# Taking the wide elementwise work off GpSimd in a two-block chain: splits and convolution on VectorE, stick-breaking masks by matmul, the gated branch first

## The chip, the cores and the metric

The kernel runs on one core of a Trainium2 chip. The metric is device time in microseconds (us). Before the change the median of three runs is 1020.0 us (1019.26 to 1021.23). A profile records one execution on the chip, instruction by instruction, for the engines PE (TensorE; PEld is its weight load), DVE (VectorE), ACT (ScalarE), POOL (GpSimd) and SP (SyncE, which issues the DMAs).

## The reference, cut to what matters

Two blocks over 256 tokens of width 1024, in fp32. The first is a mixing layer with a feed-forward layer; the second has a retention layer and a differential attention layer, each with a convolutional feed-forward layer. The change touches the mixing layer, and the way in which all weights are prepared.

```python
h = _rmsnorm(x, g_attn)
p = h @ w_in            # columns: a_b, a_c, a_h (256 each), b_glu (512), q, k, v (512 each)
y_a = a_b * _causal_dwconv(a_c * a_h, w_conv_a)                       # 3 taps
g = b_glu[..., :256] * jax.nn.sigmoid(b_glu[..., 256:])
g = _causal_dwconv(g, w_conv_b) + b_conv_b                            # 31 taps
y_b = jax.nn.silu(_layernorm(g, ln_b_g, ln_b_b))
# stick-breaking attention, 8 heads of 64, for each block of 128 queries:
z = einsum(q, k) * scale
mask = s_idx < t_idx
log_beta = log_sigmoid(z)
log_1m = where(mask, log_beta - z, 0.0)
suffix = cumsum(log_1m, reverse) - log_1m
a = where(mask, exp(log_beta + suffix), 0.0)
y_c = a @ v
x = x + concatenate([y_a, y_b, y_c]) @ w_out
```

## The kernel before

**Weights and matmuls.** All weights are packed into 322 units of 128 x 1024 numbers, loaded in pairs by SP into `raw`. Each unit is split into two fp32r parts: ACT copies it to `hi`, and `raw - hi` becomes `lo` (`split_one`, lines 374 to 397). The products are formed as hi·hi + hi·lo + lo·hi, three matmuls for each. A ring of 8 unit pairs (`RING`) holds split units; a unit's slot is free again when its last matmul has been issued. A unit comes in one of three forms: `ws` (the weights are stationary, 256 tokens move: 24 matmuls of 256 columns, result as [channel, token]; `wstat`, line 520), `xs` (activations stationary, 512 weight columns move, result as [token, channel]; four units make 512 columns, 48 matmuls of 512 columns; `xstat_tokens` and `xstat`, lines 550 to 572) and `kt` (the down projections, also 512 columns; `Down`, line 588).

**The order of instructions.** `Flow` (lines 147 to 213) is a planner that runs when the kernel is built. Each operation has a priority (CHAIN, ATT, EVAC, SPLIT, IDLE, MAIN, in this order) and an estimated cost in ns; whenever an engine is free by these estimates it takes the most urgent operation whose inputs are there. The instructions are then fixed in that order: on the chip each engine runs its list strictly in order. All vector, scalar and matmul instructions are recorded through line 200 (`kick` calls them at line 200), so the views have to be read by tile names.

**Who makes `lo`.** By `split_one`, DVE makes it with one subtraction of 1024 columns (two of 512 while a phase border is being crossed or in the fine part of the attention), unless DVE's backlog by the plan is larger than POOL's by a margin (`SPILL` 1200 ns, `HELD_SPILL` -1500 ns, `FINE_SPILL` 0); then POOL makes it in four pieces of 256 columns. 28 of the units go to POOL.

**The mix phase** (`mix_phase`, line 645) takes 22 units of `w_in` in this order: V (four `xs` units), GLU (four `ws` units, two channel blocks), four head pairs (`q` and `k`, one `ws` unit each), y_a (six `ws` units); then 8 `kt` units of `w_out` in the order of `MIX_KT`: the four head pairs' channels, y_a's first, y_b's two, y_a's second. `Down` computes token block 0 for all eight, and token block 1 for seven of them afterwards (`TAIL`), while the residual and the norm of token block 0 (`chain`) are already on their way.

- *Convolution of 31 taps* (`conv_b`, `conv_pool`, lines 734 to 767): the first channel block's 31 taps and 8 of the second's are on DVE, one instruction each, with priority IDLE; 23 taps of the second block are on POOL, two instructions each (a scaled copy into `tap`, an addition into `part`). Norm (`norm`) and swish (`swish`) follow; they end with `y_ready[2]` and `y_ready[3]`.
- *Stick-breaking* (`stick`, line 821), for one pair of heads: scores into two PSUM banks (fp32 matmuls), two sigmoids on ACT to `gam` (1 - beta) and two to `beta`, in strips of 388 columns with spare columns between the blocks; POOL masks both with `affine_select` (two each) and clears one column; DVE forms the running product from the right by `tensor_tensor_scan` over `gam` and `one`, then `beta * run`; PE transposes (`at0`, `at1`), and `sb_av` multiplies with V into `yp`. `gam` and `run` exist once, `beta` twice.
- PSUM has 8 banks, handed out first come first served (`Slots`).

Each phase border has a chain of its own: residual, sum of squares (ACT), the reciprocal root by a power of -0.5 on one column (POOL, `rstd_of`, line 440), scaling (DVE, `big`), transposes, and the split of the activations.

Of the kernel before, what the change touches and what calls it, by code (L numbers as in the profile page):

```python
# [11 lines left out]
F32R = mybir.dt.float32r  # L12
AF = mybir.ActivationFunctionType
# [4 lines left out]
P = 128  # L18
# [16 lines left out]
SPILL = 1200.0  # L35
WARM = 20
HALVED = 6
POOL_TAPS = 23
HELD_CHUNKS = 2
FINE_SPILL = 0.0  # L40
URGENT = 8
HELD_SPILL = -1500.0
# [13 lines left out]
SBW = 388  # L56
COS0, SIN0, DEC0, ONE0, TRI0 = 0, 256, 512, 2048, 2048 + 2 * SBW
NCONST = TRI0 + P

MIX_KT = [4, 5, 6, 7, 0, 2, 3, 1]  # L60
# [12 lines left out]
def plan():  # L73
# [73 lines left out]
class Flow:  # L147
    """Orders the instructions: each engine takes the most urgent operation whose inputs are there,
    by estimated costs, and the instructions are traced in that order."""
# [57 lines left out]
    def backlog(self, engine):  # L207
        return max(0.0, self.free.get(engine, 0.0) - self.now) + sum(o.cost for _, _, o in self.queue.get(engine, []))

# [6 lines left out]
class Slots:  # L216
    """Counts the buffers of one tag."""
# [26 lines left out]
class Acts:  # L244
    """Activations as [channel, token], split into two parts, and when they are there."""
# [17 lines left out]
def chain_kernel(ctx: ExitStack, tc: tile.TileContext, x_in, wpack, gains, chan, small_rows, consts, out):  # L263
# [66 lines left out]
    def tp(p, pairs):  # L330
        return pe(p, 107 * len(pairs), [(nc.tensor.transpose, (dst, src, ident), {}) for dst, src in pairs])
# [42 lines left out]
    def split_one(i, src, left):  # L374
        hi, lo = unit_at[i]
        while state["hold"] is not None and i >= state["pos"] + KEEP:
            yield state["hold"]
        held = state["hold"] is not None
        n = HELD_CHUNKS if held or state["fine"] else 1
        w = D // n  # L380
        for c in range(n):
            o = act(SPLIT, hi[:, c * w:c * w + w], src[:, c * w:c * w + w], AF.Copy)
        yield o
        if flow.backlog("dve") > flow.backlog("pool") + (HELD_SPILL if held else FINE_SPILL if state["fine"] else SPILL):
            for c in range(4):
                cs = slice(c * 256, c * 256 + 256)
                o = pool(SPLIT, 690, nc.gpsimd.tensor_tensor, lo[:, cs], src[:, cs], hi[:, cs].bitcast(F32), op=ALU.subtract)
            yield o
        else:
            for c in range(n):  # L390
                cs = slice(c * w, c * w + w)
                o = tt(SPLIT, lo[:, cs], src[:, cs], hi[:, cs].bitcast(F32), ALU.subtract)
            yield o
        left[0] -= 1
        if not left[0]:
            raw.put()
        flow.fire(unit_done[i])
# [29 lines left out]
    junk = cpool.tile([P, 512], mybir.dt.bfloat16, tag="junk", name="junk")  # L427
# [92 lines left out]
    def wstat(dst, w, sx):  # L520
# [3 lines left out]
        for k in range(KD):  # L524
            if k % 4 == 0:
                yield sx.ready[0][k // 4]
                yield sx.ready[1][k // 4]
            o = pe(MAIN, 325, [
                mm(dst, h3[:, k, :], sx.hi[:, k, :], k == 0, False),
                mm(dst, h3[:, k, :], sx.lo[:, k, :], False, False),  # L530
                mm(dst, l3[:, k, :], sx.hi[:, k, :], False, k == KD - 1)])
            yield o.end
# [3 lines left out]
    def xstat_mm(dst, u, j, t, sx):  # L536
        hi, lo = u
        tsl = slice(t * P, (t + 1) * P)
        for kk in range(2):
# [3 lines left out]
            o = pe(MAIN, 645, [  # L543
# [30 lines left out]
    def down_mm(acc, n, i, t, u, y):  # L574
# [6 lines left out]
        for d, cs in ((a, c0), (b, c1)):  # L581
            o = pe(MAIN, 645, [mm(d, yh[:, tsl], hi[:, cs], first, False), mm(d, yh[:, tsl], lo[:, cs], False, False),
                               mm(d, yl[:, tsl], hi[:, cs], False, last)])
            yield o.end
            both.append(o)
# [59 lines left out]
    def mix_phase(mp):  # L645
# [25 lines left out]

        def late_loads():
            yield raw_seen2
            cop = load(ch, chan, P * NCH * 4)
            oop = load(one, consts[:, ONE0:ONE0 + 2 * SBW], P * 2 * SBW * 4)
            yield cop
            yield oop
        raw_seen2 = pair_seen[3]
# [8 lines left out]
        for beta in betas:  # L687
            nc.gpsimd.memset(beta[:, :, 386:388], 0.0)
        nc.gpsimd.memset(gam[:, :, 386:388], 0.0)
# [11 lines left out]
        yield from xstat_tokens("w_in", sx, [v_evac])  # L701

# [5 lines left out]
        sgs = slots(mp, 1, [P, S], F32, "sg")  # L708
# [9 lines left out]
        glus = []  # L718
        for c in range(2):
            p0, p1 = yield from banks.get(2)  # L720
            yield from wstat(p0[:, :S], "w_in", sx)
            o = yield from wstat(p1[:, :S], "w_in", sx)
            glus.append(flow.spawn(glu(c, p0, p1, o)))
# [3 lines left out]
        part = mp.tile([P, S], F32, tag="part", name="part")  # L727
        taps = [mp.tile([P, S], F32, tag=f"tap{n}", name=f"tap{n}") for n in range(2)]

        def pool_tap(j, out, s2):  # L730
            w = ch[:, CB0 + 31 + j:CB0 + 32 + j]
            return pool(IDLE, 460, nc.gpsimd.tensor_scalar, out, gpad[:, 1, j:j + S], w, s2, op0=ALU.mult, op1=ALU.add)

        def conv_pool():
            o = pool_tap(0, part, 0.0)
            prev = None
            for j in range(1, POOL_TAPS + 1):
                if j < POOL_TAPS:
                    o = pool_tap(j, taps[j % 2], 0.0)
                if prev is not None:  # L740
                    o = pool(IDLE, 690, nc.gpsimd.tensor_tensor, part, part, prev, op=ALU.add)
                prev = taps[j % 2]
                yield o.end
            yield o

        def conv_b():
# [7 lines left out]
            started = set()  # L754
            o = None
            for c, j in todo:
                if o is not None:
                    yield o.end
                w = ch[:, CB0 + 31 * c + j:CB0 + 31 * c + j + 1]
                if c not in started:  # L760
                    started.add(c)
                    o = ts(IDLE, cb[:, c, :], gpad[:, c, j:j + S], w, ch[:, BB0 + c:BB0 + c + 1], ALU.mult, ALU.add)
                else:
                    o = stt(IDLE, cb[:, c, :], gpad[:, c, j:j + S], w, cb[:, c, :], ALU.mult, ALU.add)
            yield o
            yield other
            yield tt(EVAC, cb[:, 1, :], cb[:, 1, :], part, ALU.add)
# [40 lines left out]
        def sb_av(i, j, at, yp, beta, v_ok):  # L808
            cs = slice(j * 64, j * 64 + P)
            yield tp(ATT, [(at[:, b * P:(b + 1) * P], beta[:, j, c0:c0 + P]) for b, c0 in enumerate((0, 130, 258))])  # L810
# [10 lines left out]
        def stick(i, pr):  # L821
# [3 lines left out]
            scs = yield from banks.get(2)  # L825
            sops = []
            for j in range(2):
                rows = slice(j * 64, j * 64 + 64)
                sops.append(pe(ATT, 650, [mm(scs[j][:, 0:130], q[rows, 0:P], k[rows, 0:130], True, True),
                                          mm(scs[j][:, 130:386], q[rows, P:S], k[rows, :], True, True)]))  # L830
            yield from bgr.get()
            beta = yield from bbeta.get()
            for j in range(2):
# [3 lines left out]
                a = act(ATT, gam[:, j, 0:386], scs[j][:, 0:386], AF.Sigmoid, scale=-0.125)  # L837
                b = act(ATT, beta[:, j, 0:386], scs[j][:, 0:386], AF.Sigmoid, scale=0.125)
            yield a

            def mask(tile_, b0, fill):
                return pool(ATT, 362, nc.gpsimd.affine_select, out=tile_[:, :, b0:b0 + P], in_=tile_[:, :, b0:b0 + P],
                            pattern=[[0, 2], [-1, P]], compare_op=ALU.is_gt, fill=fill, base=0, channel_multiplier=1)

            g_ops = [mask(gam, 0, 1.0), mask(gam, 258, 1.0), pool(ATT, 100, nc.gpsimd.memset, gam[:, :, 128:129], 0.0)]
            yield b
            banks.put(2)
            b_ops = [mask(beta, 0, 0.0), mask(beta, 258, 0.0)]
# [3 lines left out]
            for o in g_ops:  # L852
                yield o
            yield consts_in
# [4 lines left out]
            for o in b_ops:  # L859
                yield o  # L860
# [18 lines left out]
        for i in range(4):  # L879
# [6 lines left out]
            flow.spawn(stick(i, pr))  # L886

# [561 lines left out]
def _constants():  # L1449
# [14 lines left out]
    for h in range(2):  # L1464
        c[:, ONE0 + h * SBW + 128] = 1.0
        c[:, ONE0 + h * SBW + 386] = 1.0
    q = np.arange(P)
    c[:, TRI0:TRI0 + P] = np.where(q[None, :] <= q[:, None], 0.0, -1e30)
    return c
# [26 lines left out]
```

## Time and profile before

| | |
|---|---|
| median of three runs | 1020.0 us |
| span of the profiled execution, first to last instruction | 1016.7 us |
| mean granted TensorE clock | 0.990 |
| DVE `lo<-raw,hi` 128x1024 | 288 x 1245 ns |
| POOL `lo<-raw,hi` 128x256 | 112 x 1021 ns |
| POOL `tap<-gpad,ch` and `part<-part,tap` | 22 x 1063 ns and 22 x 873 ns |
| POOL masks of `gam` and of `beta` | 8 x 424 ns and 8 x 1136 ns |
| DVE scan `run<-gam,one` | 4 x 1945 ns |

The profiled execution has no time of its own beside its span; the span lies 3.3 us under the median of the runs. In the page, the busy share of an engine is an average over the whole span. A line of the timeline has the start, the duration, the engine, the line, the operation, output<-inputs and, in brackets, the idle time of the engine before it and what ended that. A matmul's duration is longer than the step to the next one, since matmuls are pipelined: PE's pace is read from starts.

### The profile page before, as it was taken

To read this page: it belongs to the slowest core of one execution; us is meant where nothing else is said; L and a number is where in the kernel's file an instruction comes from. 1 tells how busy PE (TensorE), PEld (TensorE's weight loads), DVE (VectorE), ACT (ScalarE), POOL (GpSimd) and SP (SyncE) were. 2 spreads that over 40 slices of the span, in tenths; PEclk is the share of its full clock that TensorE was granted. 3 is DMA by queue.
4 is the path that set the end of the run, shared out by engine and by line. 5 is a ranking of instruction groups with operands and counts; after the bars stand their busy time and mean duration, and the time that the engine had idled before them with its cause. 6 is when DMAs were issued, how large, how long until landed. Compare 5 with 4: busy or idle time off the path is not lost.

```text
span 1016.7 us, 15598 instructions
## 1 busy us (share of the span) xinstructions
PE 986.9 (97%) x6144; PEld 880.4 (87%) x6144; DVE 688.9 (68%) x1010; ACT 561.3 (55%) x948; POOL 191.4 (19%) x232
## 2 busy tenths in 40 slices
PE   8977999999999999999999999999999999999997
PEld 6966878999997989898879999998899779999996
DVE  5798666555557676565379866666777579766663
ACT  5633456444435545445368555556767768555551
POOL 1497060000007010000062100005200262100000
PEclk9978999999999999999999999999999999999999
DMA  8712347455544744545347555553653246555531
GB/s 299 284 43 90 139 166 289 169 205 171 201 167 162 273 134 174 199 154 178 135 166 269 208 171 203 172 202 129 206 212 125 83 166 228 208 174 199 172 119 42
DMA packets 28441, 180.07 MB, mean 177 GB/s; under 512 B 3152, under 2 KB 4304, under 8 KB 8528
## 3 DMA queue, kind: packets, MB, share of 16 engines
q1 hardware_dynamic: 28368, 179.08, 49.8%
q8 instruction: 48, 0.79, 0.3%
q14 instruction: 25, 0.20, 0.1%
HBM read 178.02 MB, written 1.05 MB: 176 GB/s over the span
## 4 chain that ended last, share of the span: by engine, by line
PE 67%; issue 18%; POOL 9%; DVE 2%; ACT 1%; DMA 1%; SPq 0%; POOLq 0%; DVEq 0%; ACTq 0%
PE bank L200 67%; POOL lo L200 5%; POOL tap L200 2%; POOL part L200 1%; POOL tiny L200 1%; DMA raw<-wpack 1%; ACT hi L200 1%; DVE lo L200 1%; POOL beta L200 0%; DVE big L200 0%; DVE run L200 0%; POOL gam L200 0%; ACT junk L200 0%; DVE x L200 0%; DVE beta L200 0%
## 5 line engine op out<-in xcount | busy, mean ns | idle before, releaser
L200 DVE TENSOR_TENSOR lo<-raw,hi 128x1024 fp32r<-128x1024 f32 (+1 forms) x300 | 369.8, 1238 | 129.7 <-ACT hi L200 129.0
L200 ACT ACTIVATE hi<-raw 128x1024 fp32r<-128x1024 f32 (+1 forms) x344 | 340.5, 1002 | 144.6 <-PE bank L200 125.7
L200 PE MATMUL bank<-xh,hi 128*128 128x256 f32 x1104 | 316.2, 286 | 0.0
L200 PE MATMUL bank<-xh,lo 128*128 128x256 f32 x1104 | 313.3, 284 | 0.0
L200 PE MATMUL bank<-xl,hi 128*128 128x256 f32 x1104 | 313.2, 284 | 0.0
L200 PEld LDWEIGHTS bank<-xh,hi 128*128 128x128 f32 x1104 | 212.6, 193 | 3.9 <-issue 1.3
L200 PEld LDWEIGHTS bank<-xl,hi 128*128 128x128 f32 x1104 | 212.5, 192 | 2.5
L200 PEld LDWEIGHTS bank<-xh,lo 128*128 128x128 f32 x1104 | 212.3, 192 | 0.0
L200 POOL TENSOR_TENSOR tiny<-tiny,mhalf 128x1 f32<-128x1 f32 (+1 forms) x40 | 25.1, 629 | 708.7 <-DVE tiny L200 708.7
L200 POOL TENSOR_TENSOR lo<-raw,hi 128x256 fp32r<-128x256 f32 x112 | 110.7, 1021 | 86.4 <-ACT hi L200 85.0
L200 PE MATMUL bank<-hi,xh 128*128 128x512 f32 x272 | 108.2, 398 | 0.0
L200 DVE SCALAR_TENSOR_TENSOR cv<-bank,ch,cv 128x254 f32<-128x254 f32 (+1 forms) x176 | 72.5, 474 | 51.8 <-ACT cv L200 51.6
L200 PE MATMUL bank<-lo,xh 128*128 128x512 f32 x272 | 106.5, 391 | 0.8 <-DVE lo L200 0.8
L200 PE MATMUL bank<-hi,fh 128*128 128x512 f32 x272 | 106.9, 393 | 0.0
L200 PE MATMUL bank<-hi,xl 128*128 128x512 f32 x272 | 106.7, 392 | 0.1
L200 PE MATMUL bank<-lo,fh 128*128 128x512 f32 x272 | 106.5, 392 | 0.0
L200 PE MATMUL bank<-hi,fl 128*128 128x512 f32 x272 | 105.9, 389 | 0.0
L200 ACT ACTIVATE cv<-bank,ch 128x256 f32<-128x256 f32 x88 | 44.2, 561 | 61.7 <-PE bank L200 61.7
L200 PEld LDWEIGHTS bank<-lo,xh 128*128 128x128 f32 x272 | 51.2, 188 | 12.0 <-DVE lo L200 1.9
L200 PEld LDWEIGHTS bank<-hi,xl 128*128 128x128 f32 x272 | 51.1, 188 | 12.0 <-DVE xl L200 1.4
L200 PEld LDWEIGHTS bank<-hi,fl 128*128 128x128 f32 x272 | 51.1, 188 | 11.0
L200 PEld LDWEIGHTS bank<-hi,xh 128*128 128x128 f32 x272 | 51.2, 188 | 9.7 <-ACT xh L200 0.2
(170 smaller groups left out, 1188.9 us busy)
## 6 DMA issues: line engine op xcount, KB each, us to landing
raw<-wpack SPq DMA_DIRECT2D x155, 1024.0 KB, 4.9
big<-gains SPq DMA_DIRECT2D x12, 512.0 KB, 6.7
raw<-wpack SPq DMA_DIRECT2D x12, 512.0 KB, 7.5
x<-x SPq DMA_DIRECT2D x4, 256.0 KB, 5.8
out_dram<-x SPq DMA_DIRECT2D x4, 256.0 KB, 2.1
dec<-consts SPq DMA_DIRECT2D x4, 192.0 KB, 5.2
one<-consts SPq DMA_DIRECT2D x1, 388.0 KB, 6.0
ch<-chan SPq DMA_DIRECT2D x1, 213.5 KB, 5.5
```

The lines of the kernel that those rows point to most:

```text
L200: fn(*a, **k)
```

## The change

- *Splits*: every `lo` is made on DVE; the choice between DVE and POOL, with its margins and `backlog`, is gone.
- *Order of `w_in`*: GLU is first and now has the form `xs` (512 columns, result as [token, channel]); V comes after the second head pair (`V_AFTER = 1`) and uses `xstat`, which holds two banks.
- *GLU*: sigmoid and product for each token block, then two PE transposes and an ACT copy into `gpad`; two buffers `sg` instead of one.
- *Convolution*: all 62 taps on DVE, channel blocks in turn.
- *Masks*: after each pair's scores, a bf16 matmul of an identity with a tile that has 0 below the diagonal and -1e30 on and above it adds the mask to the scores' two diagonal blocks in PSUM. The sigmoids then give 1 for `gam` and 0 for `beta` there. Strips are 384 columns wide; the scan's second operation is `max`, with ones at the blocks' ends. POOL's masks and clears are gone.
- *Costs in the plan*: a group of three 256-column matmuls 358 ns instead of 325, of three 512-column matmuls 681 instead of 645, the scan 1860 instead of 880, transposes 96 each and 90 more instead of 107 each.

POOL keeps the powers of one or two columns and the clears at the start.

```diff
 def plan():
-    xs("w_in", 2304)
-    for c in (768, 1024, 896, 1152):
-        ws("w_in", c)
+    xs("w_in", 768)
     for i in range(4):
         ws("w_in", 1280 + i * P)
         ws("w_in", 1792 + i * P)
+        if i == V_AFTER:
+            xs("w_in", 2304)
...
 def split_one(i, src, left):
-        if flow.backlog("dve") > flow.backlog("pool") + (HELD_SPILL if held else FINE_SPILL if state["fine"] else SPILL):
-            for c in range(4):
-                cs = slice(c * 256, c * 256 + 256)
-                o = pool(SPLIT, 690, nc.gpsimd.tensor_tensor, lo[:, cs], src[:, cs], hi[:, cs].bitcast(F32), op=ALU.subtract)
-            yield o
-        else:
-            for c in range(n):
+        for c in range(n):
+            cs = slice(c * w, c * w + w)
+            o = tt(SPLIT, lo[:, cs], src[:, cs], hi[:, cs].bitcast(F32), ALU.subtract)
+        yield o
...
-        def glu(c, p0, p1, o):
+        def glu(t, d, o):
             yield o
             sg = yield from sgs.get()
-            yield act(EVAC, sg, p1[:, :S], AF.Sigmoid)
-            yield tt(EVAC, gpad[:, c, 30:], p0[:, :S], sg, ALU.mult)
-            banks.put(2)
+            yield act(EVAC, sg, d[:, S:], AF.Sigmoid)
+            yield tt(EVAC, sg, d[:, :S], sg, ALU.mult)
+            banks.put()
+            pt = yield from banks.get()
+            yield tp(EVAC, [(pt[:, c * P:(c + 1) * P], sg[:, c * P:(c + 1) * P]) for c in range(2)])
             sgs.put()
+            yield act(EVAC, gpad[:, :, 30 + t * P:30 + (t + 1) * P], pt[:, :S].rearrange("p (c s) -> p c s", c=2), AF.Copy)
...
         def conv_b():
-            other = flow.spawn(conv_pool())
-            todo = [(0, j) for j in range(31)]
-            for n, j in enumerate(range(POOL_TAPS, 31)):
-                todo.insert(3 * n + 1, (1, j))
+            for j in range(31):
+                for c in range(2):
...
         def stick(i, pr):
+            yield consts_in
             for j in range(2):
-                sops.append(pe(ATT, 650, [mm(scs[j][:, 0:130], q[rows, 0:P], k[rows, 0:130], True, True),
-                                          mm(scs[j][:, 130:386], q[rows, P:S], k[rows, :], True, True)]))
+                pe(ATT, 435, [mm(scs[j][:, 0:P], q[rows, 0:P], k[rows, 0:P], True, False),
+                              mm(scs[j][:, P:SBW], q[rows, P:S], k[rows, :], False, False)])
+            for j in range(2):
+                diag = scs[j].rearrange("p (b c) -> p b c", b=2)[:, :, 0:P]
+                sops.append(pe(ATT, 130, [mm(diag, identb, trib.rearrange("p (a c) -> p a c", a=1).broadcast_to([P, 2, P]), False, True)]))
...
-            g_ops = [mask(gam, 0, 1.0), mask(gam, 258, 1.0), pool(ATT, 100, nc.gpsimd.memset, gam[:, :, 128:129], 0.0)]
-            b_ops = [mask(beta, 0, 0.0), mask(beta, 258, 0.0)]
-            yield flow.op("dve", ATT, 880, [(nc.vector.tensor_tensor_scan, (rf[:, ::-1], gf[:, ::-1], one[:, ::-1], 0.0),
-                                             {"op0": ALU.mult, "op1": ALU.add})])
+            s_op = flow.op("dve", ATT, 1860, [(nc.vector.tensor_tensor_scan, (rf[:, ::-1], gf[:, ::-1], one[:, ::-1], 0.0),
+                                             {"op0": ALU.mult, "op1": ALU.max})])
```

More of the change, by code (lines that the diff above doesn't have):

```diff
@@ L330, in tp @@
     def tp(p, pairs):
-        return pe(p, 107 * len(pairs), [(nc.tensor.transpose, (dst, src, ident), {}) for dst, src in pairs])
+        return pe(p, 96 * len(pairs) + 90, [(nc.tensor.transpose, (dst, src, ident), {}) for dst, src in pairs])
     def split_to(p, hi, lo, src):
@@ L377, in split_one @@
             yield state["hold"]
[L378 to L379 removed]
+        n = HELD_CHUNKS if state["hold"] is not None or state["fine"] else 1
         w = D // n
@@ L670, in mix_phase @@
         one = mp.tile([P, 2 * SBW], F32, tag="one", name="one")
+        tri = mp.tile([P, P], F32, tag="tri", name="stri")
         def late_loads():
@@ L675, in late_loads @@
             oop = load(one, consts[:, ONE0:ONE0 + 2 * SBW], P * 2 * SBW * 4)
+            top = load(tri, consts[:, TRI0 + P:TRI0 + 2 * P], P * P * 4)
             yield cop
             yield oop
+            yield top
+            act(EVAC, identb, ident, AF.Copy)
+            yield act(EVAC, trib, tri, AF.Copy)
         raw_seen2 = pair_seen[3]
@@ L686, in mix_phase @@
         bbeta = Slots(flow, 2, lambda: free_betas.pop(0))
-        for beta in betas:
-            nc.gpsimd.memset(beta[:, :, 386:388], 0.0)
-        nc.gpsimd.memset(gam[:, :, 386:388], 0.0)
+        trib = mp.tile([P, P], BF16, tag="trib", name="trib")
+        identb = mp.tile([P, P], BF16, tag="identb", name="identb")
         vp = mp.tile([P, 2, 4, 192], F32, tag="vp", name="vp")
@@ L707, in mix_phase @@
         nc.gpsimd.memset(gpad[:, :, 0:30], 0.0)
-        sgs = slots(mp, 1, [P, S], F32, "sg")
-        def glu(c, p0, p1, o):
+        sgs = slots(mp, 2, [P, S], F32, "sg")
+        glus = [Ev(), Ev()]
+        def glu(t, d, o):
             yield o
             sg = yield from sgs.get()
-            yield act(EVAC, sg, p1[:, :S], AF.Sigmoid)
-            yield tt(EVAC, gpad[:, c, 30:], p0[:, :S], sg, ALU.mult)
-            banks.put(2)
-            sgs.put()
[L718 to L723, printed above, removed]
+            yield act(EVAC, sg, d[:, S:], AF.Sigmoid)
[3 more added lines that the diff above has]
+            yield tp(EVAC, [(pt[:, c * P:(c + 1) * P], sg[:, c * P:(c + 1) * P]) for c in range(2)])
+            sgs.put()
+            yield act(EVAC, gpad[:, :, 30 + t * P:30 + (t + 1) * P], pt[:, :S].rearrange("p (c s) -> p c s", c=2), AF.Copy)
+            banks.put()
+            flow.fire(glus[t])
+        yield from xstat_tokens("w_in", sx, [glu])
         cb = mp.tile([P, 2, S], F32, tag="cb", name="cb")
         xn = gpad[:, :, 0:S]
[L727 to L744, printed above, removed]
         def conv_b():
@@ L836, in stick @@
                     qks.put(2)
[L837 to L843, printed above, removed]
-            g_ops = [mask(gam, 0, 1.0), mask(gam, 258, 1.0), pool(ATT, 100, nc.gpsimd.memset, gam[:, :, 128:129], 0.0)]
-            yield b
-            banks.put(2)
-            b_ops = [mask(beta, 0, 0.0), mask(beta, 258, 0.0)]
+                a = act(ATT, gam[:, j, :], scs[j][:, 0:SBW], AF.Sigmoid, scale=-0.125)
+                b = act(ATT, beta[:, j, :], scs[j][:, 0:SBW], AF.Sigmoid, scale=0.125)
             gf = gam.rearrange("p j c -> p (j c)")
```

61 lines of the change are left out of this document (25 added, 36 removed).

## The prediction

> **What bounds the kernel now.** I read the page first: the span, the busy shares, the granted clock by slices and the chain that ended last.
>
> ```profile
> span 1016.7 us, 15598 instructions
> PE 986.9 (97%) x6144; PEld 880.4 (87%) x6144; DVE 688.9 (68%) x1010; ACT 561.3 (55%) x948; POOL 191.4 (19%) x232
> ...
> PEclk9978999999999999999999999999999999999999
> ...
> PE 67%; issue 18%; POOL 9%; DVE 2%; ACT 1%; DMA 1%; SPq 0%; POOLq 0%; DVEq 0%; ACTq 0%
> ```
>
> PE carries the kernel, and its clock dips in one place, the third and fourth of 40 slices. POOL, busy for a fifth of the span, holds 9% of the chain. Next, the stages of the mix phase by busy time:
>
> ```profile
> 25.96:38.26 12.30, 12.30 (x104) 12.30 (x104) 7.85 (x8) 8.81 (x11) 0.00 (x0) 1.00 0.90 309
> 38.26:98.20 59.94, 45.98 (x321) 42.07 (x320) 52.98 (x63) 25.48 (x47) 54.30 (x65) 0.86 0.30 108
> ...
> 110.98:123.60 12.62, 12.62 (x57) 10.16 (x56) 5.83 (x11) 2.43 (x3) 0.00 (x0) 1.00 0.50 202
> 123.60:145.00 21.40, 20.85 (x101) 16.71 (x100) 15.22 (x20) 13.83 (x25) 17.47 (x18) 1.00 0.45 154
> ```
>
> The columns are PE, PEld, DVE, ACT, POOL, clock, DMA. From 38.26 (first convolution tap) to 98.20 (last) PE is idle for 14.0 of 59.94 us, while POOL (54.30) and DVE (52.98) are almost full. The waits of 40 to 100 us, and one head pair in the timelines of PE and DVE, show why:
>
> ```profile
> PE bank L200 <- DVE beta L200: 14.0, 4, 4.6
> ...
> DVE run L200 <- POOL gam L200: 6.2, 4, 2.2
> ```
>
> ```profile
> 50.68 0.93 PE L200 MATMUL bank<-qk,qk 64*128 64x130 f32 x8
> 55.44 1.54 PE L200 MATMUL bank<-ident,beta 128*128 128x128 f32 x6 [3.83 <-DVE beta L200]
> ```
>
> ```profile
> 51.29 1.94 DVE L200 TENSOR_TENSOR_SCAN run<-gam,one 128x776 f32<-128x776 f32 x1 [1.39 <-POOL gam L200]
> 53.15 1.35 DVE L200 TENSOR_TENSOR lo<-raw,hi 128x1024 fp32r<-128x1024 f32 x1
> 54.43 0.95 DVE L200 TENSOR_TENSOR beta<-beta,run 128x775 f32<-128x775 f32 x1
> ```
>
> The scan waits for the masks, which POOL makes between its taps, the product for the scan, and the transposes, put into PE's order by a planner that charges 880 ns for a scan of 1.94 us, hold up every weight matmul behind them. Four such holes are all of the 14.0 us. The clock of 0.86 means that 28% of 59.94 us, 16.8 us, went by at half speed.
>
> **PE's share of the stage.** The steps of PE at full clock, from its timeline: 29 matmuls of 512 columns (19.21 to 25.57), 153 of 256 columns (25.79 to 44.02), scores, and a stretch of six transposes, nine weight matmuls and eight value matmuls (95.87 to 98.96):
>
> ```profile
> 19.21 0.39 PE L200 MATMUL bank<-lo,xh 128*128 128x512 f32 x1
> 25.57 0.39 PE L200 MATMUL bank<-hi,xl 128*128 128x512 f32 x1
> 25.79 0.28 PE L200 MATMUL bank<-xh,hi 128*128 128x256 f32 x1
> ```
>
> ```profile
> 44.02 0.28 PE L200 MATMUL bank<-xh,lo 128*128 128x256 f32 x1
> 44.23 0.93 PE L200 MATMUL bank<-qk,qk 64*128 64x130 f32 x8
> 45.10 0.38 PE L200 MATMUL bank<-xh,hi 128*128 128x256 f32 x1
> ```
>
> ```profile
> 95.87 0.88 PE L200 MATMUL bank<-ident,beta 128*128 128x128 f32 x6 [2.80 <-DVE beta L200]
> 98.96 0.60 PE L200 MATMUL bank<-ident,cb 128*128 128x128 f32 x4
> 99.31 0.36 PE L200 MATMUL bank<-xh,hi 128*128 128x256 f32 x1
> ```
>
> A start-to-start step is 6.36/28 = 0.227 us for 512 columns and 18.23/152 = 0.120 for 256; a pair's scores cost 0.87, its transposes and values 3.09 - 9 x 0.120 = 2.0, four transposes 0.35. The stage from 25.79 to the first `w_out` matmul at 110.98 lasts 85.2 us. Its work at full speed is 18 units x 24 x 0.120 = 51.8, four pairs x 2.9 = 11.6, eight later transposes 0.7: 64.1 us. So 21 us are lost here, 14.0 in holes and about 7 to the half clock.
>
> Changed, GLU takes V's place ahead of 25.79. Behind it stand 14 units x 2.88 = 40.3, V as four 512-column units 48 x 0.227 = 10.9, pairs 11.6, eight mask matmuls of 256 columns, GLU's four transposes 0.35 and 0.7. The masks are in bf16, which the trace doesn't show: 0.120 each by the f32r row, up to 0.22 by the fp32 scores (eight matmuls of 128 and 256 columns in 0.87); I take 0.120, 1.0 in all. Sum 64.9: the floor for the start of `w_out` is 90.7, a gain of 20.3. ACT, busy for 25.48 of 59.94 us, has room for V's moved evictions and GLU's new copy. One hole I expect: V wants two banks while two pairs hold three each (`at0`, `at1`, `yp`), that is all eight, and `q` of pair 2 is queued behind V's eviction. I put 1.5 us there (0 to 3): 92.2.
>
> **DVE's share.** What it must do until the convolution is done decides the rest. Its rows between 26 and 124 us, then taps (four of the same kind, in the conv phase, POOL idle) and splits back to back without POOL beside them:
>
> ```profile
> L200 DVE TENSOR_TENSOR lo<-raw,hi 128x1024 fp32r<-128x1024 f32 x23 | 29.5, 1297 | 4.4 <-ACT hi L200 4.4
> L200 DVE SCALAR_TENSOR_TENSOR cb<-gpad,ch,cb 128x256 f32<-128x256 f32 x37 | 25.7, 715 | 0.4
> ```
>
> ```profile
> 579.93 1.65 DVE L200 SCALAR_TENSOR_TENSOR cv<-bank,ch,cv 128x255 f32<-128x255 f32 x4 [1.67 <-ACT cv L200]
> 581.50 1.21 DVE L200 TENSOR_TENSOR lo<-raw,hi 128x1024 fp32r<-128x1024 f32 x1
> ```
>
> ```profile
> 33.11 3.50 DVE L200 TENSOR_TENSOR lo<-raw,hi 128x1024 fp32r<-128x1024 f32 x3 [0.52 <-ACT hi L200]
> 37.92 0.42 DVE L200 TENSOR_TENSOR gpad<-bank,sg 128x256 f32<-128x256 f32 x1 [1.31 <-ACT sg L200]
> 38.26 0.40 DVE L200 TENSOR_SCALAR cb<-gpad,ch 128x256 f32<-128x256 f32 x1
> ```
>
> A tap costs 0.715 us beside POOL and 1.57/4 = 0.39 alone: the 62 taps on DVE alone cost 24.2 us, less than the 25.7 that 37 cost now. POOL's share of the convolution was paid by slowing DVE. Alone, a split costs (3.50 - 1.21)/2 = 1.14.
>
> The first tap now starts at 38.26. With GLU ahead its last matmul starts at 25.57; product, transposes and a copy follow, an estimate of 28.5. From there to the last tap DVE does: taps 24.2; about 21 splits (23 between 26 and 124 now, none of them POOL's) 23.9; four scans x 1.86 (51.29 to 53.15) 7.4; four products x 0.95 = 3.8; `yl` and half of conv_a, ten small steps at 0.35 (an estimate between taps and the 0.42 row), 3.5. Sum 62.8. Now DVE is busy for 52.98 of 59.94 and waits 6.2 for POOL, 99% together; I allow 95%, so 66 us: last tap at 94.6. Then the normalisation. Its DVE rows now:
>
> ```profile
> 97.78 0.42 DVE L200 TENSOR_TENSOR cb<-cb,part 128x256 f32<-128x256 f32 x1
> ...
> 107.13 0.41 DVE L200 TENSOR_TENSOR yl<-cb,yh 128x256 fp32r<-128x256 f32 x1
> ...
> 109.72 0.41 DVE L200 TENSOR_TENSOR yl<-cb,yh 128x256 fp32r<-128x256 f32 x1
> ```
>
> From the end of `cb` (98.20) 9.3 us to the first half, 11.9 to the second. With two `sg` buffers the halves come closer: 104.0 and about 106. `w_out` begins at 92.2 and wants them in its sixth and seventh of eight steps, after (12.62/9) x 6 = 8.4 us, at 100.6; so PE waits 3.4 for the first and about 1 for the second, and then does three steps of 1.4: the token-0 pass, now over at 123.60, ends at 109.2. Gain 14.4; I take 14.5. DVE has taken PE's place as what ends this stage last, and moved V, masks and transposes sit under it.
>
> **Outside the mix phase.** 28 units' splits move from POOL to DVE, 28 x 1.14 = 31.9 us, nearly all at the phase borders. There, these rows (POOL's pow and DVE's product after it, minimum/median/maximum; PE's wait for the product after 100 us; one pow and the split beside it):
>
> ```profile
> L200 POOL TENSOR_TENSOR tiny<-tiny,mhalf x40: 540/550/1532, 5.3 to 1011.6; 128x1 f32<-128x1 f32 x32, 128x2 f32<-128x2 f32 x8
> ...
> L200 DVE SCALAR_TENSOR_TENSOR big<-x,tiny,big x28: 737/751/1229, 8.7 to 831.3; 128x512 f32<-128x512 f32 x28
> ```
>
> ```profile
> PE bank L200 <- DVE big L200: 3.9, 9, 1.0
> ```
>
> ```profile
> 518.95 1.29 DVE L200 TENSOR_TENSOR lo<-raw,hi 128x1024 fp32r<-128x1024 f32 x1
> ```
>
> ```profile
> 519.12 1.53 POOL L200 TENSOR_TENSOR tiny<-tiny,mhalf 128x1 f32<-128x1 f32 x1
> ```
>
> The chain loses its queue behind POOL splits, and its products go from 1.23 towards 0.74. What DVE gains in work has room: in 123.60 to 145.00 it is idle for 6.2 us, and four units there cost 4.6. So the cover holds, and the gain is bounded by PE's wait: 0 to 3.9. Without the cover it would be up to 31.9 of loss. I take 1.5 of gain. The scan's and PE's corrected costs change the order elsewhere too; PE waits for nothing in the long middle stretches, so nothing for that. The mask matmuls wait for `tri`, a new 64 KB load on SP behind `one`, and for two small copies on ACT; behind them on PE are weight matmuls, but the first scores, at about 38 us, come long after SP's constants, which the first tap already uses at 38.26: nothing.
>
> Sum: 14.5 + 1.5 = 16.0 us off the profiled span. That span is 3.3 us under the median of 1020.0, outside the first and last instruction, and unchanged. 1020.0 - 16.0 = 1004.0.
>
> **Rivals.** *DVE is later than I think.* At 85% the last tap ends at 28.5 + 73.9 = 102.4, the first half at 111.7, the pass at 116.9: a gain of 6.7 and 1.5, 1011.8. For it: nothing but 5% of slack stands in my ledger. The half clock could come back too: four waits of at most 4.6 us went with 16.8 us of it, so even my wait of 3.4 us may halve the clock for what follows it, three steps of 1.4: up to 4.2 us, inside the range. The Trainium skill (TensorE: Matmul & The Clock Gate, HAM oscillation) puts the limit at idle gaps of about 3.4 us; the holes of 2.80 and 3.83 us in this stretch neither confirm nor refute it. *PE is the only bound.* The taps finish in time, all borders gain: 20.3 - 0 + 3.9, 996. Against it: DVE's ledger.
>
> *The pow is blocked by the splits.* Row 519.12: a pow that started 0.17 us into a split took 1.53 instead of 0.55. With every border split on DVE, each of 18 border pows (four at four borders, two at the first) could pay 0.98, 17.6 us in all; PE's held-back token-1 work covers about half of them (the token-0 chains): 9, so 1013. The Trainium skill (SBUF — State Buffer, Who interferes with whom) says that a DVE instruction with two SBUF inputs and a GpSimd instruction reading SBUF exclude each other, the first to start holding the ports to its end. The 1.53 us row agrees with that. Against the price: the median of the 40 pows is 0.55, though DVE splits at the borders now too.
>
> *Slower: the border splits stand ahead of the chain.* DVE takes them in order, in pieces as long as a chain step; if over half of the 31.9 us lies open, the whole gain is gone; all of it gives 1004 + 32 = 1036. Against it: the idle 6.2 us above and the chain's higher priority. *No change*: PE's holes come back under another name (DVE's scan now waits for taps), 1020.
>
> **How the numbers follow.** Forecast (1000 to 1008) 0.50, late DVE 0.21, PE alone 0.11, pow 0.08, border splits 0.07, no change 0.03. The range 997 to 1014 leaves out the last two and the edge of PE alone and the pow. About 0.2% (2 us) is what a measurement here can tell: faster 0.88, same 0.04, slower 0.08.
>
> **What would show it.** In the changed profile: no PE wait on `beta` over 1 us and a full clock from 40 to 90; taps at 0.39 to 0.48; `w_out` starting near 92 and a wait of PE for `yl` or `yh` of 2 to 5 us near 100; POOL under 40 us busy; border pows mostly at 0.55. The forecast is wrong if taps stay near 0.7, if PE waits over 8 us for y_b, or if the phase borders together lengthen by more than 5 us.

## The result, and the profile after

The changed kernel takes 994.56 us (median of four runs, 993.63 to 995.56) against 1019.84 for the kernel before (with a fourth run; 1019.26 to 1021.23): a ratio of 0.9751 [0.9739, 0.9763], 25.3 us faster. Forecast were 1004.0 us and a range of 997 to 1014. The direction was right; the gain is 9.3 us larger than the 16.0 forecast, and the time lies 2.4 us under the range. The page of the changed kernel (its vector, scalar and matmul instructions are recorded at line 198):

```profile
span 993.8 us, 15342 instructions
PE 980.7 (99%) x6108; PEld 876.1 (88%) x6108; DVE 689.3 (69%) x1076; ACT 562.5 (57%) x952; POOL 30.2 (3%) x52
...
PEclk9999999999999999999999999999999999999999
...
PE 92%; DVE 2%; ACT 2%; issue 2%; DMA 1%; POOL 1%; SPq 0%; DVEq 0%; POOLq 0%; ACTq 0%
```

POOL's work fell from 191 to 30 us, and DVE's busy time did not grow (688.9 to 689.3), though it took over 28 units' splits and 23 taps. Why, the rows under d_spare_pool show. The clock's dip is gone, and PE holds 92% of the chain that ended last instead of 67%. Next, the stages by busy time, from the first tap to the end of the last and then `w_out`'s first pass (columns: PE, PEld, DVE, ACT, POOL, clock, DMA share, GB/s):

```profile
31.46:90.42 58.96, 58.96 (x440) 54.36 (x440) 58.65 (x100) 34.58 (x59) 0.00 (x0) 1.00 0.48 165
92.24:104.90 12.66, 12.66 (x60) 10.47 (x59) 8.51 (x21) 4.40 (x7) 1.19 (x3) 1.00 0.41 151
```

PE is never idle in either, at full clock; DVE is full until the last tap, 58.65 of 58.96 us. DVE's groups between 31.40 and 90.42 us:

```profile
L198 DVE SCALAR_TENSOR_TENSOR cb<-gpad,ch,cb 128x256 f32<-128x256 f32 x60 | 25.5, 474 | 0.0
L198 DVE TENSOR_TENSOR lo<-raw,hi 128x1024 fp32r<-128x1024 f32 x20 | 24.1, 1215 | 0.3 <-ACT hi L198 0.2
L198 DVE TENSOR_TENSOR_SCAN run<-gam,one 128x768 f32<-128x768 f32 x4 | 7.0, 1750 | 0.0
L198 DVE TENSOR_TENSOR beta<-beta,run 128x767 f32<-128x767 f32 x4 | 3.8, 948 | 0.0
```

A tap takes 474 ns where it took 715 beside POOL, a scan 1750 where it took 1945. How the end of the convolution meets `w_out`, from DVE's and PE's timelines:

```profile
31.46 0.73 DVE L198 TENSOR_SCALAR cb<-gpad,ch 128x256 f32<-128x256 f32 x2
...
36.91 1.75 DVE L198 TENSOR_TENSOR_SCAN run<-gam,one 128x768 f32<-128x768 f32 x1
38.58 1.20 DVE L198 TENSOR_TENSOR lo<-raw,hi 128x1024 fp32r<-128x1024 f32 x1
...
89.16 1.26 DVE L198 SCALAR_TENSOR_TENSOR cb<-gpad,ch,cb 128x256 f32<-128x256 f32 x3
...
98.03 0.41 DVE L198 TENSOR_TENSOR yl<-cb,yh 128x256 fp32r<-128x256 f32 x1
...
98.70 0.41 DVE L198 TENSOR_TENSOR yl<-cb,yh 128x256 fp32r<-128x256 f32 x1
```

```profile
92.24 0.40 PE L198 MATMUL bank<-hi,yh 128*128 128x512 f32 x1
...
100.92 0.39 PE L198 MATMUL bank<-hi,yh 128*128 128x512 f32 x1
```

The last tap ends at 90.42, y_b's first half is ready at 98.44, and `w_out`'s 37th matmul at 100.92 is the first that reads it: 2.5 us to spare. PE's transposes on the way there had less: those of `cb` start at 90.73, 0.3 us after the last tap, and those of `gpad` at 95.00, 0.7 after their input (94.34). At the borders, PE's weight loads waited for the product behind the power like this, before (first) and after, between 115 and 1008 us:

```profile
PEld bank L200 <- DVE big L200: 7.8, 11, 1.5
```

```profile
PEld bank L198 <- DVE big L198: 2.2, 5, 0.7
```

### The profile page after: what moved, and what is told of

It is laid out like the page before. It is cut to its first block, busy times and chain, and to the rows that moved or that the text cites. A ratio compares the mean times of both kernels' runs of the same rounds, so it can differ in the third digit from the quotient of the medians.

```text
span 993.8 us, 15342 instructions
## 1 busy us (share of the span) xinstructions
PE 980.7 (99%) x6108; PEld 876.1 (88%) x6108; DVE 689.3 (69%) x1076; ACT 562.5 (57%) x952; POOL 30.2 (3%) x52
## 4 chain that ended last, share of the span: by engine, by line
PE 92%; DVE 2%; ACT 2%; issue 2%; DMA 1%; POOL 1%; SPq 0%; DVEq 0%; POOLq 0%; ACTq 0%
PE bank L198 92%; ACT junk L198 1%; DVE lo L198 1%; DMA big<-gains 1%; POOL tiny L198 1%; DVE x L198 1%; DVE big L198 0%; ACT hi L198 0%; ACT L198 0%; DVE tiny L198 0%; ACT pe L198 0%; ACT aT L198 0%; DVE xl L198 0%; ACT dyh L198 0%; SPq L198 0%
## 5 line engine op out<-in xcount | busy, mean ns | idle before, releaser
L198 DVE TENSOR_TENSOR lo<-raw,hi 128x1024 fp32r<-128x1024 f32 (+1 forms) x344 | 393.7, 1153 | 129.7 <-ACT hi L198 128.5
L198 PE MATMUL bank<-xh,hi 128*128 128x256 f32 x1072 | 306.1, 286 | 0.0
L198 PE MATMUL bank<-xh,lo 128*128 128x256 f32 x1072 | 303.3, 283 | 0.0
L198 PE MATMUL bank<-xl,hi 128*128 128x256 f32 x1072 | 303.3, 283 | 0.0
L198 PEld LDWEIGHTS bank<-xh,hi 128*128 128x128 f32 x1072 | 205.4, 192 | 3.7 <-issue 1.0
L198 PEld LDWEIGHTS bank<-xl,hi 128*128 128x128 f32 x1072 | 205.4, 192 | 2.6
L198 PEld LDWEIGHTS bank<-xh,lo 128*128 128x128 f32 x1072 | 205.3, 191 | 0.0
L198 PE MATMUL bank<-lo,xh 128*128 128x512 f32 x288 | 112.4, 390 | 0.2 <-DVE lo L198 0.2
L198 PEld LDWEIGHTS bank<-hi,xh 128*128 128x128 f32 x288 | 54.1, 188 | 10.4
L198 PEld LDWEIGHTS bank<-hi,fh 128*128 128x128 f32 x272 | 51.3, 189 | 9.1
L198 PEld LDWEIGHTS bank<-lo,fh 128*128 128x128 f32 x272 | 51.3, 189 | 8.5
```

Source lines behind the costliest of these rows:

```text
L198: fn(*a, **k)
```

## The experiments

Theory L: POOL's wide operations slow DVE's while both run, by about as much as they relieve it, in a way that the fixed order can't foresee; PE, strictly in order, then waits. Rival P: the plan's wrong costs (scan 880, transposes) put PE's transposes too early, and the corrected costs are the gain. A third question is what bounds the changed mix phase: PE alone, or still DVE's convolution.

Stages are read from starts of matmuls in each timeline: from the first of 256 columns, behind V or GLU, to the first of `w_out`; from the first to the last of `w_out`; from the first feed-forward matmul to the end of the span. Each ratio is to the kernel before on the same chip, whose median there was 1019.6 to 1020.3 us.

| kernel | us | ratio to before [95%] | to `w_out` | `w_out` | rest |
|---|---|---|---|---|---|
| before | 1019.84 | | 85.2 | 23.1 | 882.4 |
| after | 994.56 | 0.9751 [0.9739, 0.9763] | 64.6 | 23.0 | 878.3 |
| a_pool_splits | 1006.91 | 0.9876 [0.9861, 0.9891] | 66.2 | 23.0 | 888.8 |
| a_pool_taps | 1011.65 | 0.9920 [0.9904, 0.9937] | 81.8 | 22.5 | 878.4 |
| a_v_first | 1002.01 | 0.9828 [0.9814, 0.9843] | V ahead | 30.9 | 878.4 |
| b_new_costs | 1025.34 | 1.0057 [1.0041, 1.0073] | 84.7 | 23.1 | 888.3 |
| c_before_dve_splits | 1012.85 | 0.9935 [0.9917, 0.9952] | 86.5 | 23.1 | 875.6 |
| c_after_old_costs | 993.49 | 0.9745 [0.9730, 0.9759] | 64.8 | 24.7 | 875.5 |
| c_pool_masks | 997.05 | 0.9779 [0.9764, 0.9793] | 65.8 | 23.6 | 878.5 |
| c_half_taps | 997.61 | 0.9786 [0.9771, 0.9800] | 67.7 | 22.5 | 878.4 |
| d_spare_pool | 1008.85 | 0.9889 [0.9871, 0.9907] | 77.8 | 23.0 | 878.5 |
| d_short_conv | 994.58 | 0.9753 [0.9738, 0.9768] | 65.4 | 22.5 | 878.3 |
| d_mixed_costs | 999.84 | 0.9806 [0.9791, 0.9821] | 64.0 | 30.6 | 875.5 |
| d_scan_add | 994.76, one run | | 64.6 | 23.0 | 878.4 |
| e_phase_costs | 992.84 | 0.9736 [0.9721, 0.9750] | 64.6 | 23.0 | 875.5 |
| e_phase_groups | 991.34 | 0.9719 [0.9702, 0.9735] | 64.6 | 23.0 | 874.6 |
| e_spare_splits | 1009.36 | 0.9899 [0.9885, 0.9914] | 64.6 | 23.0 | 893.0 |

**a_pool_splits**: the changed kernel with the old choice between DVE and POOL.

```diff
-        for c in range(n): ... o = tt(SPLIT, lo[:, cs], ...)
+        if flow.backlog("dve") > flow.backlog("pool") + (...): four pieces on POOL
+        else: on DVE
```

> The changed kernel with one part undone: the choice of DVE or POOL for the splits, with its margins, is back; all else as changed. Theory L (POOL's wide work beside DVE costs DVE as much as it relieves, and the border chains queue behind POOL's splits): the stages after the mix phase become 3 to 5 us longer, so about 998.5 us, with DVE products at 1.2 us and pows behind splits at the borders. Rival P (the borders gained because the planner's PE costs are now right): no change, 994 to 995.5.

12.4 us over the changed kernel, 10.4 of them behind the mix phase: the border splits on POOL cost over twice the 3 to 5 us expected, though only 24 units go to POOL here, instead of 28 before (96 pieces instead of 112).

**a_pool_taps**: the changed kernel with 23 taps back on POOL.

```diff
+POOL_TAPS = 23
-            for j in range(31): for c in range(2): ... on DVE
+            other = flow.spawn(conv_pool())
```

> The changed kernel with the old convolution: 23 taps of the second channel block on POOL, 39 on DVE. Theory L: the 39 taps on DVE go back from 0.39 to about 0.65 us a step, the scans from 1.75 to about 1.94, so the last tap comes no earlier than now (90.4 us) and 3 to 8 us later; y_b has only about 2.5 us of slack, so 995 to 1001 us. Rival (POOL's taps were a real relief and only the masks and the order hurt): the last tap 5 us or more earlier, time unchanged at 994 to 995.

PE's wait of 26 to 110 us, and the scan's durations, minimum/median/maximum:

```profile
PE bank L199 <- DVE beta L199: 12.3, 2, 9.1
```

```profile
L199 DVE TENSOR_TENSOR_SCAN run<-gam,one x4: 1748/1910/2298, 39.4 to 89.8; 128x768 f32<-128x768 f32 x4
```

With POOL's taps alone, and with the corrected costs, the holes are back: at 1011.65 us, 17.1 over the changed kernel and past the 995 to 1001 us expected, with a mean clock of 0.90 from the first 256-column matmul to `w_out`. One of the four scans takes 2298 ns, another 1748. DVE's 39 taps were expected to end later than the 62 of the changed kernel (90.4 us) and ended at 83.6; what came late were the products that PE's transposes read. The old order of DVE's taps came back too, in which many read the tap before them; d_spare_pool is free of that.

**a_v_first**: the changed kernel with V ahead of GLU again.

```diff
+    xs("w_in", 2304)
     xs("w_in", 768)
...
-        if i == V_AFTER:
-            xs("w_in", 2304)
```

> The changed kernel with V in front again, GLU second (still in the token form), all else as changed. Theory S (the early start of the convolution is needed, since DVE has only about 2.5 us to spare): the taps start 10.9 us later and end about 8 to 10 us later, PE waits for y_b, 1000 to 1003 us. Rival (the order of GLU and V hardly matters, PE's holes were the masks and the scan): 994 to 996 us.

DVE starts its taps later, and the wait that the prediction expected of the changed kernel appears here. PE's waits of 80 to 125 us, in y_b's normalisation:

```profile
PE bank L197 <- DVE gpad L197: 2.3, 2, 2.1
PE bank L197 <- ACT yh L197: 2.2, 1, 2.2
```

With the waits and the clock behind them (0.67 from 103 to 112 us) `w_out` lasts 7.9 us longer. GLU's place ahead of V is worth 7.5 us.

**b_new_costs**: the kernel before with the corrected costs and nothing else.

```diff
-pe(MAIN, 325, ...  pe(MAIN, 645, ...  107 * len(pairs)  scan 880
+pe(MAIN, 358, ...  pe(MAIN, 681, ...  96 * len(pairs) + 90  scan 1860
```

> The kernel before with nothing but the planner's corrected costs (matmul groups, transposes, scan); POOL keeps its work. Theory P (the holes were the planner's error: it charged 880 ns for a scan of 1945): PE's four waits for beta shrink from 14.0 us to under 4 and the clock stays up, 1002 to 1008 us. Rival L (POOL's queue and the slowed DVE make the holes): the holes shrink by less than half, 1012 to 1019 us.

It is 5.5 us slower than the kernel before, which neither theory had. PE's wait of 26 to 110 us is as long as before the change (14.0), and the rest is 5.9 us longer: rival P fell.

```profile
PE bank L200 <- DVE beta L200: 13.9, 4, 5.0
```

**c_before_dve_splits**: the kernel before with the changed `split_one`.

> The kernel before with nothing but the splits moved to DVE; convolution, masks, order and planner's costs as before. Theory L (the border gain comes from POOL's splits going): the stages behind the mix phase, 882.4 us from the first feed-forward matmul to the end in the profile before, shrink to about 878.5; the mix phase, where POOL takes no split, stays at 85 us: 1015 to 1017 us. Rival (the splits on POOL did no harm under the old costs, they only hurt together with the new ones): no change, 1019 to 1020.5.

7.2 us faster, more than expected. By the stages the rest is 6.8 us shorter and the mix phase 1.3 longer. The border product there, before and in this kernel, between 115 and 1010 us:

```profile
L200 DVE SCALAR_TENSOR_TENSOR big<-x,tiny,big 128x512 f32<-128x512 f32 x24 | 22.6, 964 | 10.4 <-POOL tiny L200 10.4
```

```profile
L200 DVE SCALAR_TENSOR_TENSOR big<-x,tiny,big 128x512 f32<-128x512 f32 x24 | 17.6, 747 | 4.3 <-POOL tiny L200 4.3
```

The same 24 products take 22.6 us beside POOL's splits and 17.6 without, and DVE's wait for the power falls from 10.4 to 4.3. Splits and costs do not add up: POOL's splits cost 6.8 us behind the mix phase with the old costs and 10.4 with the corrected ones (a_pool_splits); the corrected costs lose 5.9 us there with POOL's splits (b_new_costs) and 2.8 without (c_after_old_costs).

**c_after_old_costs**: the changed kernel with all old costs.

> The changed kernel with the planner's old costs (scan 880, matmul groups 325 and 645, transposes 107 each). Theory L (with POOL out of the way the estimates are close, and an error of 0.9 us in four scans gives four holes of about 1 us and an early order elsewhere): 997 to 1000 us. Rival P (the corrected costs are most of the gain in the mix phase): over 1004 us, holes of 3 us and more per pair.

The expected loss did not come: it is 1.1 us faster than the changed kernel, with intervals that overlap. No hole of the old size came back with a scan charged at 880: PE waited 0.2 us for a product of the pairs and 0.9 for y_b. The rest is 2.8 us shorter than in the changed kernel, `w_out` 1.7 longer.

**c_pool_masks**: the changed kernel with its masks on POOL by `affine_select`, no mask matmuls.

> The changed kernel with the masks made by POOL (affine_select, planned at 420 ns) on the 384-column strips instead of by matmul; POOL has no other wide work. Theory L (masks on POOL hurt since they queue behind taps and are slowed beside DVE; alone they hurt little): two masks of gam at 0.4 stand ahead of each scan, two of beta run beside it; holes under 1.5 us per pair, the DVE order slips by about 1 us per pair and y_b loses its slack: 996 to 1000 us. Rival M (the masks themselves made the holes): 1003 us or more.

2.5 us slower, as theory L had it: the masks alone are little of the gain. With them as POOL's only wide work the scan's median is 1933 ns, near the 1945 before.

**c_half_taps** and **d_short_conv**: fewer taps, to see whether DVE still bounds the mix phase.

```diff
-            for j in range(31):
+            for j in range(31):     # c_half_taps: for c in range(2 if j == 0 else 1)
+            for j in range(16):     # d_short_conv: for c in range(2)
```

> The changed kernel without 30 of the 31 taps of the second channel block, so that part of the convolution is left out and DVE is relieved of 11.7 us in the mix phase. Theory B (PE alone bounds the changed mix phase; DVE has slack): 994 to 995 us, no change. Rival D (DVE still ends the stage, as the prediction had it): 3 to 5 us faster, 990 to 991.5.

> The changed kernel with 16 instead of 31 taps in both channel blocks, so that part of the convolution is left out; the blocks still take turns. DVE is relieved of 30 x 0.39 = 11.7 us. Theory B (PE alone bounds the changed mix phase): 993.5 to 995 us, no change. Rival D (DVE still ends the stage): 990 to 991.5 us.

With 30 taps fewer, c_half_taps was 3.1 us slower, which no theory had: on one channel block each tap reads the tap before it, two such stand 0.52 us apart where the plan charges 0.40, and the transposes of `cb` were placed too early. PE's timeline:

```profile
60.66 0.28 PE L198 MATMUL bank<-xh,lo 128*128 128x256 f32 x1
63.51 0.63 PE L198 MATMUL bank<-ident,cb 128*128 128x128 f32 x4 [2.56 <-DVE cb L198]
```

So it didn't decide the question. d_short_conv did, with both blocks and 16 taps each: DVE has room (52.13 of 60 us), and the time is that of the changed kernel. PE alone bounds its mix phase.

```profile
30.00:90.00 60.00, 59.97 (x447) 55.09 (x447) 52.13 (x84) 36.16 (x63) 1.15 (x4) 1.00 0.47 164
```

**d_spare_pool**: the changed kernel; POOL does 46 spare operations during the convolution that nothing waits for.

```diff
+            for j in range(23):
+                o = pool(IDLE, 460, nc.gpsimd.tensor_scalar, dtap[j % 2], dsrc, ...)
+                o = pool(IDLE, 690, nc.gpsimd.tensor_tensor, dsum, dsum, dtap[j % 2], ...)
```

> The changed kernel with work added to POOL that nothing depends on: 23 scaled copies and 23 additions of 128x256 on buffers of their own, the size and kind of the old convolution taps, from the moment the convolution starts; DVE still does all 62 taps. Theory L (POOL's wide operations slow DVE's two-input operations merely by running beside them, and PE, whose order is fixed, then waits): taps at 0.6 to 0.7 us a step while POOL works, scans over 1.9 us, holes in front of the transposes: 1003 to 1012 us. Rival (only what waits for POOL can lose time): 994 to 995.5 us.

14.3 us slower, without a single dependence on POOL's added work; the stage before `w_out` alone is 13.2 us longer, at a mean clock of 0.91. The scan, and PE's wait of 26 to 110 us:

```profile
L198 DVE TENSOR_TENSOR_SCAN run<-gam,one x4: 1741/1852/2280, 40.8 to 85.4; 128x768 f32<-128x768 f32 x4
```

```profile
PE bank L198 <- DVE beta L198: 8.2, 2, 4.2
```

The wait is 8.2 us; the other 5.0 are PE busy for longer at the lower clock (69.62 us instead of 64.63). A stretch of DVE's and POOL's timeline shows how the two slow each other:

```profile
50.04 0.61 DVE L198 SCALAR_TENSOR_TENSOR cb<-gpad,ch,cb 128x256 f32<-128x256 f32 x1
50.46 0.78 POOL L198 TENSOR_TENSOR dsum<-dsum,dtap 128x256 f32<-128x256 f32 x1
50.57 2.28 DVE L198 TENSOR_TENSOR_SCAN run<-gam,one 128x768 f32<-128x768 f32 x1
51.20 1.85 POOL L198 TENSOR_SCALAR dtap<-dsrc 128x256 f32<-128x256 f32 x1
```

They take turns. Each of the last three starts while the other engine is still at work, and ends only when its own work fits in behind that: POOL's addition 0.59 us after the tap's end, the scan 1.61 after the addition's, POOL's copy 0.20 after the scan's. So a duration, and the busy time of an engine, holds its waiting for the other one; this is why DVE's busy time did not grow when it took POOL's work. The Trainium skill (SBUF — State Buffer, Who interferes with whom) says that a DVE operation with two SBUF inputs excludes a GpSimd operation that reads SBUF. The rows agree. The means (a tap's goes from 474 to 562 ns, a scan's from 1750 to 1932) mix two kinds: the 16 taps that started while POOL worked took 0.61 or about 0.95 us, the other 44 took 0.45 to 0.48.

**d_scan_add**: the scan's second operation is `add` again.

> The changed kernel with add instead of max as the scan's second operation, so that the running product is not reset as it should be and the attention weights differ; the instruction's size is the same. Theory L (the scan was slowed by POOL's masks beside it: 1945 ns before, 1750 now): it stays at 1750 ns. Rival (max is the faster operation): 1920 to 1945 ns.

```profile
L198 DVE TENSOR_TENSOR_SCAN run<-gam,one x4: 1742/1745/1759, 36.1 to 72.2; 128x768 f32<-128x768 f32 x4
```

The scan stays at 1745 ns: the 1945 before were POOL's doing and not the operation's (with POOL's masks on the same narrower strips, c_pool_masks, it was back at 1933).

**d_mixed_costs**: old costs of matmuls and transposes, the scan at 1860.

> The changed kernel with the old planner's costs for matmul groups and transposes, and the new one (1860) for the scan. Theory C (the old PE costs order the phase borders and the differential attention better by 2.8 us, the scan's true cost keeps the mix phase free of holes): 991.5 to 993 us, faster than the changed kernel and at least as fast as with all old costs. Rival: the two orders differ only by chance and the sum is anywhere between 993 and 996 us.

5.3 us slower than the changed kernel, outside both forecasts. The rest was short as hoped, but the plan put taps behind other work: they end at 99.7, and `w_out` waits. PE's timeline, and the window after it:

```profile
99.35 0.94 PE L198 MATMUL bank<-ident,cb 128*128 128x128 f32 x4
102.41 1.42 PE L198 MATMUL bank<-ident,gpad 128*128 128x128 f32 x4 [2.11 <-DVE gpad L198]
105.87 0.79 PE L198 MATMUL bank<-hi,yh 128*128 128x512 f32 x1 [2.04 <-ACT yh L198]
```

```profile
106.00:112.00 6.00, 6.00 (x21) 4.83 (x22) 1.59 (x4) 0.41 (x2) 0.00 (x0) 0.76 0.00 0
```

With a_v_first this shows a second time how thin the 2.5 us are.

**e_phase_costs** and **e_phase_groups**: the corrected costs in the mix phase, old ones behind it.

```diff
             yield from mix_phase(mp)
+        cost.update(ws=325, xs=645, tp=107, tp0=0)    # e_phase_costs
+        cost.update(ws=325, xs=645)                   # e_phase_groups
```

> The changed kernel; the corrected costs of matmul groups, transposes and scan hold until the mix phase is over, and from there on the old costs (325, 645 and 107 for each transpose) hold. Theory P: in the mix phase the corrected costs are harmless now that PE alone bounds it (64.6 and 23.0 us), and behind it the old costs give an order that is 2.8 us shorter (875.5 us as in c_after_old_costs): 991 to 992.5 us, the fastest of all. Rival: the order behind the mix phase depends on where the planner's clock stands when that phase ends, and the 2.8 us are an accident of that order: 994 to 995.

> As e_phase_costs, but behind the mix phase only the matmul groups have the old costs (325 and 645); the transposes keep the corrected one (96 each and 90 more). If the groups' costs make the 2.8 us, this runs as e_phase_costs, 991 to 992.5; if the transposes' cost makes them, as the changed kernel, 994 to 995.

Both keep 64.6 and 23.0 us in the mix phase and shorten the rest, by 2.8 and 3.7 us: it is the matmul groups' cost that makes it, and the transposes' corrected cost does no harm. (Of the two, only e_phase_groups has an interval clear of the changed kernel's.) By what change in the order was not settled. Two stretches hold 2.7 of the 3.7 us, the first 28 us behind the mix phase (28.04, then 27.31) and one from 684 to 771 us (86.98, then 85.01); in the changed kernel PE and its weight loads wait behind the mix phase for at most 0.8 us at a time. e_phase_groups is the fastest version, 28.3 us under the kernel before on its chip.

**e_spare_splits**: the changed kernel, with 64 spare subtractions on POOL at the borders.

```diff
+        if state["hold"] is not None and i > 60:
+            for c in range(4):
+                pool(SPLIT, 690, nc.gpsimd.tensor_tensor, sdst, ssrc, ssrc, op=ALU.subtract)
```

> The changed kernel; at the four phase borders behind the mix phase POOL also does 16 spare subtractions of 256 columns each, on a tile of its own that nothing depends on (64 in all, as many as 16 units' splits). DVE still makes every real split. Theory B (a split on POOL costs at a border by slowing DVE's products and by standing ahead of the pow in POOL's queue): the four borders grow by 3 to 7 us together, 997.5 to 1001.5. Rival U (what cost there was that the unit itself was late, made at 1.0 us for a quarter): no growth, 994 to 995.

14.8 us slower, all behind the mix phase, though every unit is still split on DVE: the rival fell, and the cost was twice the upper end of what I expected. DVE at one border, here and in the changed kernel, and PE's weight loads:

```profile
688.39 1.10 DVE L198 TENSOR_TENSOR lo<-raw,hi 128x512 fp32r<-128x512 f32 x1
689.41 1.10 DVE L198 SCALAR_TENSOR_TENSOR big<-x,tiny,big 128x512 f32<-128x512 f32 x1
```

```profile
680.27 0.69 DVE L198 TENSOR_TENSOR lo<-raw,hi 128x512 fp32r<-128x512 f32 x1
680.87 0.75 DVE L198 SCALAR_TENSOR_TENSOR big<-x,tiny,big 128x512 f32<-128x512 f32 x1
```

```profile
PEld bank L198 <- DVE big L198: 13.0, 11, 2.0
PEld bank L198 <- DVE lo L198: 3.9, 4, 1.5
```

A product of 0.75 us takes 1.10 beside POOL, and so does a split of 0.69. Slower splits also made some units late (the wait for `lo`). Powers stood in POOL's queue too (four of them 1.09 to 2.86 us late), so the ways are not told apart; together they are the cost of a wide operation on POOL at a border.

## Why the prediction was right and wrong, step by step

**PE's floor of the stage** (64.9): right, 64.63 measured. The bank hole of 1.5 at V did not come; its stated bounds held 0. That `w_out` starts at 92.24, where 92.2 was forecast, is luck: the hole was missing, and this execution began its weight matmuls 1.8 us later.

**Taps and POOL**: right. That POOL's share of the convolution was paid by slowing DVE is shown by a_pool_taps and, without any dependence, by d_spare_pool; no wait on `beta` is left.

**DVE's ledger, and from it y_b's lateness: this step failed.** Forecast were 66 us from first tap to last; it was 58.96. Two terms make up nearly all of it. The splits: 21 were put there at 23.9 us, 18 ran there, 20.4 us at 1.135 a step (the 20 of the row above count one that began before the first tap and one that began in the last). The 5% of idle time: 3.2 us without a row, of which 0.3 came. The scan's 1.86 came from a row with POOL's masks and taps beside it; alone its step is 38.58 - 36.91 = 1.67, 0.7 us for the four. The normalisation took 8.0 and 8.7 us (90.42 to 98.44 and 99.11) instead of 9.3 and about 11.4: in the stretch of before that these prices come from, DVE waited 1.6 us for a power and for ACT, in the changed kernel 0.2. So y_b was 2.5 us early instead of 3.4 late, and the 4.4 us of waits fell away. The rival "PE is the only bound" was the case, and stood at 0.11. I had argued that removing POOL makes a tap cheaper, and then priced the scan from a row that POOL had slowed. The expected wait is a real one: it came as soon as the 2.5 us were taken (a_v_first, d_mixed_costs).

**The borders** (1.5 us, bounded by 3.9): two terms, both mis-sized. The splits' move was worth 6.8 us behind the mix phase (c_before_dve_splits). The bound was read from PE's row alone; the wait of its weight loads, 7.8, was the row to take. The corrected costs, put at nothing because PE waits for nothing in the long middle stretches, cost 2.8 us there (c_after_old_costs, e_phase_costs). Net 4.1 instead of 1.5. That PE waits for nothing in the middle did not mean that another order is free; what in the order costs it stays open.

**The pow beside splits**: the mechanism is there, 9 of 36 powers behind 100 us are long (up to 1.46 us), two before, but the sum of these 36 went from 23.0 to 26.2 us only, and the borders gained.

**Profiled span and median**: I held the 3.3 us between them constant. In the runs that list both, time and span of one execution are 2.0 to 2.2 us apart for the kernel before and 1.7 to 1.8 for the changed one (995.56 and 993.78 for the profiled run). The first matmul on weights starts at 11.58 in the one profile and 13.40 in the other; in the other runs with the changed order of GLU and V it starts anywhere from 11.0 to 14.0, so this is an offset of single executions.

Sum of the miss of 9.3: y_b's waits 4.4, the bank hole 1.5, borders 2.6, the floor 0.3; the remaining 0.5 is within what single executions differ by. The parts aren't additive: undoing splits, taps, V's place and masks one at a time costs 12.4, 17.1, 7.5 and 2.5 us, 39.5 together against a gain of 25.3.

## What to carry to other kernels

Price an operation from rows in which its neighbours are as they will be: beside a busy GpSimd a DVE row holds waiting, 715 ns for a tap of 474, 964 for a product of 747, 1945 for a scan of 1750. Count what lies in a stretch by its starts, and give idle time a row or leave it out. Work moved to an idle engine is not free because nothing waits for it; give that engine spare work that nothing depends on and see whether the time moves. Corrected costs in a planner are a change of order like any other and want a run of their own, stage by stage.

## What the runs showed of the hardware that was not expected

- 46 spare GpSimd operations that nothing waits for cost 14.3 us (d_spare_pool), 64 at the borders 14.8 (e_spare_splits).
- Two DVE taps of 256 columns that depend on each other stand 0.52 us apart, alternating ones 0.40 (c_half_taps, after).
- The clock records of the 17 traces change in steps of 3.41 us, and what they do goes by the share of such a step in which PE was busy by the profile. After every step at full clock with less than 0.43 it fell to half, after none with 0.48 or more; in between, both happened. From half it came back after steps with 0.81 or more, and not after those with 0.76 or less. A hole of 2.56 us (c_half_taps, first line) left 1.68 us busy in its emptier step, and the clock stayed at 1.00; a hole of 2.11 us behind short transposes (d_mixed_costs, second line) left 1.56, and the clock was half from 102.08 on, before that hole had ended (columns as in the stages above):

```profile
61.77:65.18 3.41, 1.68 (x15) 1.71 (x16) 3.30 (x8) 0.00 (x0) 0.00 (x0) 1.00 0.22 91
98.67:102.08 3.41, 1.56 (x8) 0.80 (x6) 2.46 (x10) 0.00 (x0) 0.85 (x2) 1.00 0.01 2
102.08:105.49 3.41, 1.38 (x4) 0.69 (x4) 2.24 (x6) 1.11 (x3) 0.21 (x1) 0.50 0.00 0
```

The Trainium skill (TensorE: Matmul & The Clock Gate, HAM oscillation) puts the limit at idle gaps of about 3.4 us; the hole of 2.11 us is below it and lost the clock all the same, and so did the hole of 3.83 us in the kernel before when it was 1.8 us old (51.61 to 53.40).
